# Receptance inputs rounded in four groups spread over the third gate block, longer landings in the recurrence's list, and row loads dealt in pairs

## The chip, the cores and the metric

The kernel runs on one core of a Trainium2 chip. The metric is the device time of one execution in microseconds. The kernel before takes 1137.41 us, the median of three runs (1137.01 to 1139.67).

## The reference

The reference is a layer of a recurrent mixer (RWKV7) followed by a layer of sparse attention, on 256 tokens of width 2048. What matters here is the mixer: six mixed inputs, four large products with weights of 2048x2048 (receptance r, key k, value v, gate z), and a recurrence of each head's 64x64 state over the tokens, with a norm, a bonus and the gate behind it.

```python
xx = token_shift(u) - u
mixed = u[None] + xx[None] * mu[:, None, None, :]
rkvz = jnp.einsum('nbtd,nde->nbte', mixed[:4], w_rkvz)
r, k, v, z = rkvz[0], rkvz[1], rkvz[2], rkvz[3]
...
o = wkv7_scan(rh, heads(decay), kh, vh, -kk, kk * ah.astype(jnp.float32))
mean = jnp.mean(o, axis=-1, keepdims=True)
var = jnp.mean(jnp.square(o - mean), axis=-1, keepdims=True)
o = ((o - mean) * lax.rsqrt(var + GN_EPS)).reshape(B, T, D) * ln_g + ln_b
bonus = jnp.sum((rh * kh * r_k).astype(jnp.float32), axis=-1, keepdims=True) * vh
o = (o + bonus.reshape(B, T, D)) * jax.nn.silu(z)
```

## The kernel before, in words

**Products in two parts.** Each float32 operand of a large product is cut into a high part rounded to the matmul's format and a low part, the rest; three matmuls add up the product. For a weight piece of 128x512, ScalarE makes the high part (`whi`, line 211) and VectorE the low part (`wlo`, line 190). The raw weights (`wraw`, 512 KB, two pieces) come through SP's queue (line 177). There are five raw tiles and five buffers each of `whi` and `wlo`, so splits run up to five pieces ahead of TensorE. A raw tile is loaded again when the low part of its last piece is made.

The mixed inputs are cut in the same way. For r, `split_into` is called sixteen times, once per block k of 128 rows: a high part of 128x256 on ScalarE (line 425, scaled by a tile that holds 1.0, `gate`) and a low part on VectorE (line 426). The gate tile is written by POOL (line 655) once the second gate block is closed, and all sixteen wait for it.

**The stages.** First come v and the small products, then k (278 us), then the gate in blocks of 512 columns: z1 until about 301 us, z2 (`late_z(2)`) until 325 us, z3 until 348 us. TensorE's order there is its own. Each block ends with `close_z`: a tanh, a scale and a product per half (lines 661 to 663) and stores of the result. From 348 us on the recurrence runs in units U = 0 to 7 of four heads, some 24 us each, and between its small matmuls the products of r (lines 1337 and 1340) fill TensorE.

**The list of the recurrence.** A planner, `Deal`, writes out the order on ScalarE, VectorE, POOL and SP by hand before anything runs. Each step has an engine, a duration, the steps it needs and a lag, the time after its end until its result counts as there. TensorE's line of steps is given; a step is due when TensorE will want what hangs on it, and an engine takes the most urgent step that can start. The order fixes what stands behind what on each queue; at run time every queue waits in order. The steps that the change touches or that are spoken of below:
- The 32x32 blocks of an inverse are made in two batches, b = 0 in an earlier stage and b = 1 on POOL, ScalarE and VectorE from 305 us until the recurrence's unit 3. Its tiles are invA, invT, invM and invX, line 823. Its results go to memory by two POOL DMAs, called `("tnd1",)` and `("yvd1",)`, which units 4 to 7 read back.
- `("a", U)`: eight POOL DMAs of 16 KB that load the rows A10 and T00 of unit U (`load_a`, lines 922 and 924). `("y", U)`: eight that load Yb (`load_y`, line 931). Each is one step, so its eight DMAs stand together.
- `("G", U)`: TensorE's first product of unit U's preparation (line 1051); needs a and y.
- S: VectorE copies the state after the first chunk (line 1151), and TensorE multiplies it with `ars` (line 1130). `st` is the statistics of a chunk (lines 1167 and 1169), `rp` POOL's power that makes 1/sqrt(var) (`rg`, line 1180), `nmr`, `v`, `b` what VectorE does with it (lines 1190 to 1194).
- SP loads `spl` (the split inputs of a unit), the rows `vt` and `zt`, `uv`, the raw weights, and three `xl` tiles of the input (line 1559), which lie where invA, invT and invX lay.

A POOL DMA's issue takes POOL's time, and a POOL queue that waits for a store's landing holds everything behind it.

Of the kernel before, what the change touches and what calls it, by code (L numbers as in the profile page):

```python
# [78 lines left out]
ZHOOK = (2, 4)  # L79
QZ = (0, 25, 24, 1, 2, 23, 22, 21, 3, 20, 19, 18, 4, 17, 16, 15, 14, 13, 12, 11, 10)  # L80
# [62 lines left out]
class Weights:  # L143


    def __init__(self, tc, pool, raw_bufs, ahead):
        self.tc = tc
        self.nc, self.pool, self.raw_bufs, self.ahead = tc.nc, pool, raw_bufs, ahead
        self.pieces, self.order, self.loads, self.raw, self.hl = [], [], [], {}, []
        self.loaded = self.split = self.taken = 0  # L150
        self.on_pool = set()
        self.kept_from, self.kept_pool = math.inf, None
        self.due, self.hold = [], False

# [47 lines left out]
    def high(self):  # L202
# [8 lines left out]
        self.nc.scalar.activation(hv, src, AF.Copy)  # L211
# [13 lines left out]
def hybrid_kernel(ctx: ExitStack, tc: tile.TileContext, a: dict, out: bass.AP):  # L225
# [320 lines left out]
    def mixgen():  # L546
        for names in (("w", "a"), ("z",), ("k",), ("r",)):
# [5 lines left out]
            for k in range(NK):  # L553
                for nm in names:
# [5 lines left out]
                    if nm == "r":  # L560
                        if k == 0:
                            yield lambda: "z1" in phase_done
                        split_into(xx[:, k, :], nm, k, gates[1.0])
# [89 lines left out]
    def gate(value):  # L653
        t = ph1.tile([128, 1], F32, name="gate", bufs=1)
        G.memset(t, value)
        gates[value] = t

# [133 lines left out]
    def phase_z1():  # L791
# [11 lines left out]
        gate(1.0)  # L803
        phase_done.add("z1")
# [113 lines left out]
    def load_a(U):  # L918
        for x in range(2):
            for h in range(2):  # L920
# [5 lines left out]
    def load_y(U, eng=G):  # L926
        for x in range(2):
            for h in range(2):
# [5 lines left out]
    def late_z(nb):  # L934
        nonlocal A10, T00, vt, zt
        ps = two()
        for k in range(NK):
            yield from rows_step(ps, "z", k, W.get(), 512)
            if nb == 3:
# [53 lines left out]
    each = [(x, h) for x in range(2) for h in range(2)]  # L993
# [414 lines left out]
    for t, nm in ((0.0, ("spl", 0, 0)), (0.0, ("spl", 0, 1)), (0.0, ("a", 0)), (3000.0, ("y", 0)), (11000.0, ("zd",))):  # L1408
        deal.end[nm] = t
# [8 lines left out]
    for i, (eng, n, fn, _) in enumerate(inv):  # L1418
        nm = ("tnd1",) if i in dones[-2:-1] else ("yvd1",) if i in dones[-1:] else ("iv", i)
        deal.end.pop(nm, None)  # L1420
        dur, lag = {"V": (vcost(n), 0.0), "S": (scost(n), 100.0), "G": (gcost(n) if n else 600.0, 100.0 if n else 3500.0),
# [3 lines left out]
    for U in range(NU):  # L1425
        add = deal.add
        e2 = later("p", U - 2, 3, 2)
        if U:
# [3 lines left out]
            if U in (1, 2):  # L1432
                add(("yz", U), "G", 530.0, lambda U=U: G.memset(Yb[U], 0.0))
            third = ("tnd1",) if U == 4 else None
            add(("a", U), "G", 4500.0, lambda U=U: load_a(U), ("Y", U - 1), third, lag=3500.0)
            add(("y", U), "G", 4500.0, lambda U=U: load_y(U), later("p", U - 3, 3, 1), ("yz", U) if U < 3 else None, ("at", 12 * min(U, 2)),
                ("yvd1",) if U == 4 else None, lag=3500.0)
# [6 lines left out]
        pe(("G", U), 600.0, lambda U=U: prep("G", U), ("a", U), ("y", U), later("M", U - 1, 0), later("M", U - 1, 1))  # L1444
# [606 lines left out]
```

## Time and profile before

| | |
|---|---|
| median of three runs | 1137.41 us |
| the profiled execution's own time | 1138.34 us |
| its span | 1136.2 us |
| TensorE busy | 1103.1 us, 97% |
| VectorE, ScalarE, POOL busy | 860.8, 714.3, 382.2 us |
| z2 and z3 | 301 to 348 us |
| recurrence with r's product | 348 to 560 us |

Times in a profile are microseconds from the start of the span. In the order of time a row gives start, duration, engine, line, operation, output<-inputs, count, and in brackets the idle time of the engine before it and what ended it. PE is TensorE, DVE VectorE, ACT ScalarE, POOL GpSimd; SPq rows are the DMA issues of SP's queue. Matmul rows overlap, so the distance between starts is what counts.

### The profile page before, as it was taken

The page shows a single profiled execution, that of the slowest core. Times are in us where ns is not written, and L with a number is a line of the kernel's source. Part 1 is how long each engine was busy: PE and PEld are TensorE (multiplying, and loading weights), DVE is VectorE, ACT ScalarE, POOL GpSimd, SP SyncE. Part 2 cuts the span into 40 slices and gives each one's busy share as a digit, 9 for nine tenths or more (in the row PEclk, how much of TensorE's full clock was granted, in tenths as well). Part 3 has the DMA queues.
Part 4 walks back from the last instruction along what each step waited for, and adds up shares of the span by engine and source line. Part 5 has one row for each costly group of instructions (what it writes and reads, how often), then busy time and mean ns, then how long its engine had stood idle before and what let it go on. Part 6 is the DMA issues. An engine that isn't in the chain of part 4 may idle for free.

```text
span 1136.2 us, 24517 instructions
## 1 busy us (share of the span) xinstructions
PE 1103.1 (97%) x8880; PEld 936.3 (82%) x8880; DVE 860.8 (76%) x1783; ACT 714.3 (63%) x1696; POOL 382.2 (34%) x488
## 2 busy tenths in 40 slices
PE   8999999999899998999999999999999999999997
PEld 6778899988677777777788888787889988898786
DVE  6999976689958996677667876674576888988564
ACT  5667688867655456565556766564656666666553
POOL 1400057755375555662010010101333435352212
PEclk9999999989999999999999999999999999999999
DMA  6568889876999968765457658585645453848562
GB/s 221 173 192 226 245 216 261 241 214 195 256 272 278 246 162 258 191 181 145 133 179 248 211 167 282 164 292 164 191 138 162 129 139 103 205 116 278 163 199 97
DMA packets 239034, 225.35 MB, mean 198 GB/s; under 512 B 58054, under 2 KB 185334, under 8 KB 238913
## 3 DMA queue, kind: packets, MB, share of 16 engines
q1 hardware_dynamic: 233472, 216.65, 65.1%
q0 software_dynamic: 5440, 7.14, 2.4%
q8 instruction: 70, 1.15, 0.4%
q14 instruction: 52, 0.42, 0.1%
HBM read 200.48 MB, written 23.10 MB: 197 GB/s over the span
## 4 chain that ended last, share of the span: by engine, by line
PE 74%; DVE 10%; DMA 7%; issue 4%; ACT 3%; POOL 1%; SPq 1%; ACTq 0%; POOLq 0%; DVEq 0%
PE bank L586 11%; PE bank L588 11%; PE bank L585 11%; PE bank L1337 5%; PE bank L610 5%; DVE wlo L190 3%; PE bank L611 3%; PE bank L604 2%; PE bank L605 2%; PE bank L606 2%; PE bank L241 2%; DMA wraw<-in_a_w_rkvz_dram 2%; PE bank L1340 2%; PE pair L1359 2%; PE pair L1361 1%
## 5 line engine op out<-in xcount | busy, mean ns | idle before, releaser
L190 DVE TENSOR_TENSOR wlo<-wraw,whi 128x512 fp32r<-128x512 f32 (+2 forms) x616 | 443.0, 736 | 164.9 <-ACT whi L211 162.3
L211 ACT ACTIVATE whi<-wraw 128x512 fp32r<-128x512 f32 (+2 forms) x664 | 399.7, 619 | 226.3 <-PE bank L588 84.9
L586 PE MATMUL bank<-wlo,mx 128*128 128x512 f32 (+3 forms) x576 | 216.2, 377 | 3.0 <-DVE wlo L190 2.0
L588 PE MATMUL bank<-whi,mx 128*128 128x512 f32 (+3 forms) x576 | 214.2, 374 | 0.0
L585 PE MATMUL bank<-whi,mx 128*128 128x512 f32 (+3 forms) x576 | 187.3, 376 | 3.6 <-ACT whi L211 2.4
L586 PEld LDWEIGHTS bank<-wlo,mx 128*128 128x128 f32 x576 | 108.3, 188 | 22.8 <-DVE wlo L190 5.5
L585 PEld LDWEIGHTS bank<-whi,mx 128*128 128x128 f32 x576 | 107.5, 188 | 21.7 <-ACT whi L211 3.5
L588 PEld LDWEIGHTS bank<-whi,mx 128*128 128x128 f32 x576 | 108.4, 188 | 16.1 <-POOL mx L1926 0.4
L1337 PE MATMUL bank<-mx,whi 128*128 128x512 f32 x256 | 101.2, 427 | 0.0
L190 POOL TENSOR_TENSOR wlo<-wraw,whi 128x512 fp32r<-128x512 f32 (+2 forms) x48 | 63.2, 1318 | 110.5 <-ACT whi L211 89.8
L610 PE MATMUL bank<-mx,whi 128*128 128x512 f32 x240 | 86.7, 397 | 0.0
L604 PE MATMUL bank<-mx,whi 128*128 128x256 f32 (+1 forms) x288 | 84.3, 293 | 0.3 <-ACT mx L425 0.3
L605 PE MATMUL bank<-mx,whi 128*128 128x256 f32 (+1 forms) x288 | 82.7, 287 | 0.0
L606 PE MATMUL bank<-mx,wlo 128*128 128x256 f32 (+1 forms) x288 | 82.5, 287 | 0.0
L586 PE MATMUL bank<-wlo,kvh 128*128 128x512 f32 x192 | 76.9, 401 | 0.0
L588 PE MATMUL bank<-whi,kvl 128*128 128x512 f32 x192 | 76.1, 396 | 0.0
L1340 PE MATMUL bank<-mx,wlo 128*128 128x256 f32 x256 | 70.4, 283 | 0.7 <-DVE wlo L190 0.7
L611 PE MATMUL bank<-mx,wlo 128*128 128x256 f32 x256 | 70.5, 285 | 0.2 <-DVE wlo L190 0.2
L585 PE MATMUL bank<-whi,kvh 128*128 128x512 f32 x192 | 67.4, 396 | 0.0
L604 PEld LDWEIGHTS bank<-mx,whi 128*128 128x128 f32 (+1 forms) x288 | 55.6, 193 | 1.3 <-ACT mx L425 0.7
L606 PEld LDWEIGHTS bank<-mx,wlo 128*128 128x128 f32 (+1 forms) x288 | 55.5, 193 | 0.8 <-DVE wlo L190 0.2
L605 PEld LDWEIGHTS bank<-mx,whi 128*128 128x128 f32 (+1 forms) x288 | 55.7, 193 | 0.5
(357 smaller groups left out, 2298.1 us busy)
## 6 DMA issues: line engine op xcount, KB each, us to landing
wraw<-in_a_w_rkvz_dram SPq DMA_DIRECT2D x128, 512.0 KB, 5.6
wraw<-in_kv_w_dram SPq DMA_DIRECT2D x48, 512.0 KB, 4.4
wraw<-in_b_w_in_dram SPq DMA_DIRECT2D x40, 512.0 KB, 4.3
wraw<-in_a_w_o_dram SPq DMA_DIRECT2D x32, 512.0 KB, 4.7
wraw<-in_b_w_o_dram SPq DMA_DIRECT2D x32, 512.0 KB, 4.1
spd<-sp SPq DMA_DIRECT2D x16, 642.0 KB, 5.0
wraw<-in_b_w_in_dram SPq DMA_DIRECT2D x24, 384.0 KB, 3.3
spl<-spd SPq DMA_DIRECT2D x14, 642.0 KB, 6.8
```

The source lines that it names most:

```text
L190: eng.tensor_tensor(lv, src, hv.bitcast(F32), op=OP.subtract)
L211: self.nc.scalar.activation(hv, src, AF.Copy)
L585: PE.matmul(o, mh[:, ts], wh[:, 0, :], start=k == ends[0], stop=False)
L586: PE.matmul(o, mh[:, ts], wl[:, 0, :], start=False, stop=False)
L588: PE.matmul(o, ml[:, ts], wh[:, 0, :], start=False, stop=k == ends[1])
L604: PE.matmul(o, wh[:, s, :], mh, start=k == 0 and first, stop=False, **kw)
L605: PE.matmul(o, wh[:, s, :], ml, start=False, stop=False, **kw)
L606: PE.matmul(o, wl[:, s, :], mh, start=False, stop=k == NK - 1, **kw)
L610: PE.matmul(o, wh[:, s, :], joint[nm, k], start=k == 0, stop=False, **kw)
L611: PE.matmul(o[:, :T], wl[:, s, :], mh, start=False, stop=False, **kw)
L1337: both = lambda: PE.matmul(o, wh[:, s, :], joint["r", k], start=k == 0, stop=k == NK - 1)
L1340: PE.matmul(o[:, :T], wl[:, s, :], mixed["r", k][0], start=False, stop=False)
```

## The change

Two parts.

**The rounding of r.** The gate tile is written by ScalarE itself (`r_gate`, an ACTIVATE of 128x1 with scale 0 and bias 1), four times. Only the sixteen blocks' first, fifth, ninth and thirteenth wait for a new gate. The first gate follows the close of z1. After steps 2, 7 and 12 of z2 the next weight split is marked: its scale is the gate tile instead of the constant 1, so that it reads the tile and the next gate must stand behind it. That gate is written after the step that follows. So z2's splits and the roundings of r are laced. ScalarE, from the close of z1; before (ten more roundings stand ahead of these rows, one after the other):

```order
L425 ACTIVATE mx_4427<-xx,gate 128x256
L425 ACTIVATE mx_4464<-xx,gate 128x256
L211 ACTIVATE whi<-wraw 128x512
L425 ACTIVATE mx_4486<-xx,gate 128x256
L425 ACTIVATE mx_4506<-xx,gate 128x256
L211 ACTIVATE whi<-wraw 128x512
L425 ACTIVATE mx_4546<-xx,gate 128x256
L425 ACTIVATE mx_4564<-xx,gate 128x256
L211 ACTIVATE whi<-wraw 128x512 x12
```

and now:

```order
L663 ACTIVATE gate<-half 128x1
L213 ACTIVATE whi<-wraw 128x512
L428 ACTIVATE mx_4183<-xx,gate 128x256
L428 ACTIVATE mx_4205<-xx,gate 128x256
L428 ACTIVATE mx_4244<-xx,gate 128x256
L213 ACTIVATE whi<-wraw,gate 128x512
L213 ACTIVATE whi<-wraw 128x512
L663 ACTIVATE gate<-half 128x1
L213 ACTIVATE whi<-wraw 128x512
L428 ACTIVATE mx_4264<-xx,gate 128x256
L428 ACTIVATE mx_4288<-xx,gate 128x256
L428 ACTIVATE mx_4305<-xx,gate 128x256
```

The twelve roundings that stood in one block are now in groups of three to five, each behind its gate, with splits between; VectorE's roundings (line 426 before, 429 now) follow in the same groups.

**The list of the recurrence.** The two stores of the inverse count as landed 6.5 us after their issue instead of 3.5. The eight loads of `("a", U)` and of `("y", U)` are four steps of two DMAs each, of 1.12 us and with a lag of 5.5 us, instead of one step of 4.5 us and a lag of 3.5; G waits for all eight steps. The list that comes out differs on ScalarE, VectorE, POOL and SP, and TensorE's is the same. POOL around 426 to 450 us; before (the tnd store and three more pairs of a and t loads stand ahead of these rows):

```order
L922 DMA a_4224<-abd 32x4x32
L924 DMA t_4225<-tnd_1541 32x4x32
L823 DMA yvd_1543<-invX 128x1024
L1042 TENSOR_TENSOR ars_4716<-spl_4704 128x384
L931 DMA Yb_4705<-yvd_1543 32x4x32 x8
L1001 MEMSET uv_4707 64x8x64 x2
L1180 TENSOR_TENSOR rg<-rg,half 128x8
```

and now:

```order
L1191 TENSOR_TENSOR rg<-rg,half 128x8
L831 DMA tnd_1541<-invT 128x1024
L831 DMA yvd_1543<-invX 128x1024
L1053 TENSOR_TENSOR ars_4722<-spl_4710 128x384
L931 DMA a_4224<-abd 32x4x32
L933 DMA t_4225<-tnd_1541 32x4x32
L931 DMA a_4224<-abd 32x4x32
L933 DMA t_4225<-tnd_1541 32x4x32
L939 DMA Yb_4711<-yvd_1543 32x4x32 x4
```

The yvd store stood behind all loads of a(4), of which the t loads wait for the tnd store; now it stands right behind that store, and Yb's loads are laced with those of a(4). VectorE at the first state of unit 3; before:

```order
L1192 TENSOR_TENSOR vt<-vt,bon 128x512
L1190 SCALAR_TENSOR_TENSOR nmr<-mv,rg 128x8
L1194 TENSOR_TENSOR vt<-vt,gb 128x512
L190 TENSOR_TENSOR wlo<-wraw,whi 128x512
L1151 COPY S<-pair_6338 128x128
L1036 TENSOR_TENSOR mb<-mb,spl_4229 128x256
L1167 BN_STATS sta<-pair_6338 128x6 x2
L1169 BN_AGGR mv<-sta 128x2 x2
```

and now:

```order
L1162 COPY S<-pair_6340 128x128
L1203 TENSOR_TENSOR vt<-vt,bon 128x512
L1201 SCALAR_TENSOR_TENSOR nmr<-mv,rg 128x8
L1205 TENSOR_TENSOR vt<-vt,gb 128x512
L1178 BN_STATS sta<-pair_6340 128x6 x2
L1180 BN_AGGR mv<-sta 128x2 x2
```

The copy S stood behind nmr, which waits for POOL's power, and stands ahead of it now. On SP the three `xl` loads, which stood behind the rows of vt and zt, two raw loads and an spl load of unit 3, stand ahead of the vt rows now; and the two copies of invM on ScalarE near z3's end stand ahead of z3's tanh instead of behind it.

```diff
--- before.py
+++ after.py
@@ -77,6 +77,7 @@
 FILLL = (3, 3, 3, 2, 3, 2, 3, 3, 3, 3, 3, 3)
 FILLO, LASTFILL = 4, 28
 ZHOOK = (2, 4)
+RGK, RGZ = (0, 4, 8, 12), (2, 7, 12)
 QZ = (0, 25, 24, 1, 2, 23, 22, 21, 3, 20, 19, 18, 4, 17, 16, 15, 14, 13, 12, 11, 10)
 SQG, XPG, W2G = 0, 1, 0
 ZB = 8
@@ -151,6 +152,7 @@
         self.on_pool = set()
         self.kept_from, self.kept_pool = math.inf, None
         self.due, self.hold = [], False
+        self.mark = {}
 
     def add(self, ap, per, queue=True):
         n, cols = ap.shape[1:]
@@ -208,7 +210,8 @@
         hv, lv = [pool.tile([128, 512], F32R, name=nm, bufs=bufs)[:, :per * cols]
                   .rearrange("p (k c) -> p k c", k=per) for nm in ("whi", "wlo")]
         eng = self.nc.gpsimd if self.split in self.on_pool else self.nc.vector
-        self.nc.scalar.activation(hv, src, AF.Copy)
+        self.nc.scalar.activation(hv, src, AF.Copy, **self.mark)
+        self.mark = {}
         self.due.append((lv, src, hv, eng))
         self.hl.append((hv, lv))
         self.raw[p][1] -= 1
@@ -558,9 +561,9 @@
                         while ("v", k) not in mixed:
                             yield 300.0
                     if nm == "r":
-                        if k == 0:
-                            yield lambda: "z1" in phase_done
-                        split_into(xx[:, k, :], nm, k, gates[1.0])
+                        if k in RGK:
+                            yield lambda: ("r", k) in phase_done
+                        split_into(xx[:, k, :], nm, k, gates["r"])
                     else:
                         mix(nm, k)
                     yield {"w": DW, "a": DW, "k": DK, "z": DZ, "r": DRM}[nm]
@@ -654,6 +657,12 @@
         t = ph1.tile([128, 1], F32, name="gate", bufs=1)
         G.memset(t, value)
         gates[value] = t
+
+    def r_gate(k):
+        t = ph1.tile([128, 1], F32, name="gate", bufs=1)
+        S.activation(t, half[:, 0:1], AF.Copy, scale=0.0, bias=1.0)
+        gates["r"] = t
+        phase_done.add(("r", k))
 
     def close_z(nb, ps, ths, eng):
         for tt in range(2):
@@ -800,8 +809,7 @@
                     if j < NK:
                         part(j)
         close_z(1, ps, [kph.tile([128, 512], F32, name="zth", bufs=2) for _ in range(2)], nc.sync)
-        gate(1.0)
-        phase_done.add("z1")
+        r_gate(RGK[0])
 
     def inverse_load(b):
         A = late.tile([128, 32, 32], F32, name="invA", bufs=1)
@@ -915,17 +923,17 @@
     inverse = lambda d, u, q: bass.AP(tensor=d.tensor, offset=d.offset + (q * 64 + u // 2 * 8 + u % 2) * 1024,
                                       ap=[[32, 32], [2 * 1024, NCH], [1, 32]])
 
-    def load_a(U):
-        for x in range(2):
-            for h in range(2):
+    each = [(x, h) for x in range(2) for h in range(2)]
+
+    def load_a(U, pairs=each):
+        for x, h in pairs:
                 j, at = 2 * U + x, 64 * (h ^ x) + 32
                 G.dma_start(A10[at:at + 32, x, :, 0:32],
                             abd[j, :, 0, 64 * h + 32:64 * h + 64, :].rearrange("c p s -> p c s"))
                 G.dma_start(T00[64 * h:64 * h + 32, x, :, 0:32], inverse(tnd[U // 4], (j % 8) * 2 + h, 0))
 
-    def load_y(U, eng=G):
-        for x in range(2):
-            for h in range(2):
+    def load_y(U, eng=G, pairs=each):
+        for x, h in pairs:
                 for q in range(2):
                     at = 64 * (h ^ x) + 32 * q
                     eng.dma_start(Yb[U % 3][at:at + 32, x, :, 32 * q:32 * q + 32],
@@ -936,6 +944,10 @@
         ps = two()
         for k in range(NK):
             yield from rows_step(ps, "z", k, W.get(), 512)
+            if nb == 2 and k in RGZ:
+                W.mark = dict(scale=gates["r"])
+            elif nb == 2 and k - 1 in RGZ:
+                r_gate(RGK[1 + RGZ.index(k - 1)])
             if nb == 3:
                 used.add(("z", k))
                 if k == ZHOOK[1]:
@@ -990,7 +1002,6 @@
     ones2 = one("ones2", [128, 2])
     PCH, PBK, OU, GY, GS, AT, XS, STA, SST, NRM = [{} for _ in range(10)]
     mm = dict(stop=True, skip_group_check=True)
-    each = [(x, h) for x in range(2) for h in range(2)]
 
     in_order = ExitStack()
     in_order.enter_context(tc.manual_schedule(engines={e.engine for e in (PE, V, S, G, nc.sync)}))
@@ -1405,7 +1416,7 @@
     def pe(nm, dur, fn, *after):
         deal.add(nm, "P", dur, fn, *after, lag=220.0)
 
-    for t, nm in ((0.0, ("spl", 0, 0)), (0.0, ("spl", 0, 1)), (0.0, ("a", 0)), (3000.0, ("y", 0)), (11000.0, ("zd",))):
+    for t, nm in ((0.0, ("spl", 0, 0)), (0.0, ("spl", 0, 1)), *[(t, (s, 0, x, h)) for t, s in ((0.0, "a"), (3000.0, "y")) for x, h in each], (11000.0, ("zd",))):
         deal.end[nm] = t
     for n in range(6, 31):
         deal.end["at", n] = 1000.0 * n
@@ -1418,7 +1429,7 @@
     for i, (eng, n, fn, _) in enumerate(inv):
         nm = ("tnd1",) if i in dones[-2:-1] else ("yvd1",) if i in dones[-1:] else ("iv", i)
         deal.end.pop(nm, None)
-        dur, lag = {"V": (vcost(n), 0.0), "S": (scost(n), 100.0), "G": (gcost(n) if n else 600.0, 100.0 if n else 3500.0),
+        dur, lag = {"V": (vcost(n), 0.0), "S": (scost(n), 100.0), "G": (gcost(n) if n else 600.0, 100.0 if n else 6500.0),
                     "Q": (1000.0, 4500.0)}[eng]
         deal.add(nm, eng, dur, fn, back, lag=lag)
         back = nm if nm != ("tnd1",) else back
@@ -1432,16 +1443,17 @@
             if U in (1, 2):
                 add(("yz", U), "G", 530.0, lambda U=U: G.memset(Yb[U], 0.0))
             third = ("tnd1",) if U == 4 else None
-            add(("a", U), "G", 4500.0, lambda U=U: load_a(U), ("Y", U - 1), third, lag=3500.0)
-            add(("y", U), "G", 4500.0, lambda U=U: load_y(U), later("p", U - 3, 3, 1), ("yz", U) if U < 3 else None, ("at", 12 * min(U, 2)),
-                ("yvd1",) if U == 4 else None, lag=3500.0)
+            for x, h in each:
+                add(("a", U, x, h), "G", 1120.0, lambda U=U, x=x, h=h: load_a(U, [(x, h)]), ("Y", U - 1), third, lag=5500.0)
+                add(("y", U, x, h), "G", 1120.0, lambda U=U, x=x, h=h: load_y(U, G, [(x, h)]), later("p", U - 3, 3, 1),
+                    ("yz", U) if U < 3 else None, ("at", 12 * min(U, 2)), ("yvd1",) if U == 4 else None, lag=5500.0)
         add(("vz", U), "G", 1050.0, lambda U=U: clear_v(U), e2)
         add(("v", U), "Q", 2300.0, lambda U=U: load_v(U), ("vz", U), ("at", 6 + 12 * min(U, 1)), lag=3000.0)
         add(("vt", U), "Q", 1600.0, lambda U=U: load_rows(vt, vd, U), ("at", 26), *[later("+", U - 1, x) for x in range(2)], lag=3000.0)
         add(("zt", U), "Q", 1600.0, lambda U=U: load_rows(zt, zd, U), ("at", 30), *[later("z", U - 1, x) for x in range(2)], lag=3000.0)
         if U % 4 == 0:
             add(("gb", U), "Q", 3600.0, lambda U=U: load_gb(U), ("at", 22), *[later(k, U - 1, x) for k in "gb" for x in range(2)], lag=3000.0)
-        pe(("G", U), 600.0, lambda U=U: prep("G", U), ("a", U), ("y", U), later("M", U - 1, 0), later("M", U - 1, 1))
+        pe(("G", U), 600.0, lambda U=U: prep("G", U), *[(s, U, x, h) for s in "ay" for x, h in each], later("M", U - 1, 0), later("M", U - 1, 1))
         add(("gs", U), "S", scost(256), lambda U=U: prep("gs", U), ("G", U), later("Y", U - 1))
         pe(("Y", U), 620.0, lambda U=U: prep("Y", U), ("gs", U))
         add(("yb", U), "S", 730.0, lambda U=U: prep("yb", U), ("Y", U))
```

## The prediction

> **What bounds the kernel now.** I read the page first, then the waits of TensorE, then the order of time around each wait.
>
> ```profile
> span 1136.2 us, 24517 instructions
> PE 1103.1 (97%) x8880; PEld 936.3 (82%) x8880; DVE 860.8 (76%) x1783; ACT 714.3 (63%) x1696; POOL 382.2 (34%) x488
> ```
>
> TensorE is busy for 1103.1 of 1136.2 us, and the change leaves its list of matmuls in the same order. Nothing can be gained but its idle time, so I looked for the idle time that lies where the change moves work. The waits of TensorE in the windows 301 to 362 us and 362 to 560 us (total, times, longest):
>
> ```profile
> PE bank L585 <- ACT whi L211: 1.9, 2, 1.3
> PE bank L1340 <- DVE wlo L190: 0.7, 1, 0.7
> ...
> PE pair L1130 <- DVE mv L1169: 3.3, 3, 2.9
> ```
>
> Three places, then: the second and third gate blocks (z2 and z3), a low part of a weight at 357 us, and one wait of 2.9 us in the recurrence.
>
> **Place one, z2 and z3.** Order of time on TensorE (start, duration, what ended the idle time):
>
> ```profile
> 306.57 0.62 PE L585 MATMUL bank<-whi,mx 128*128 128x512 f32 x2
> ...
> 307.93 0.62 PE L585 MATMUL bank<-whi,mx 128*128 128x512 f32 x2
> ...
> 310.76 0.73 PE L585 MATMUL bank<-whi,mx 128*128 128x512 f32 x2 [1.31 <-ACT whi L211]
> ...
> 312.52 0.62 PE L585 MATMUL bank<-whi,mx 128*128 128x512 f32 x2
> ...
> 323.44 0.61 PE L585 MATMUL bank<-whi,mx 128*128 128x512 f32 x2
> ...
> 325.54 0.73 PE L585 MATMUL bank<-whi,mx 128*128 128x512 f32 x2 [0.59 <-ACT whi L211]
> ...
> 327.30 0.62 PE L585 MATMUL bank<-whi,mx 128*128 128x512 f32 x2
> ```
>
> A piece of weights takes 307.93 - 306.57 = 1.36 us. From 307.93 to 312.52 lie two pieces, which should take 2.72; they took 4.59, so 1.87 us were lost. From 323.44 to 327.30 it is 3.86 - 2.72 = 1.14. The first loss is ScalarE's, which did twelve roundings in one go before the next split; the second is a late load:
>
> ```profile
> 305.28 4.91 ACT L425 ACTIVATE mx<-xx,gate 128x256 fp32r<-128x256 f32 x12 [0.68 <-POOL gate L655]
> ...
> 312.74 3.37 ACT L211 ACTIVATE whi<-wraw 128x512 fp32r<-128x512 f32 x6
> ...
> 324.86 1.15 ACT L211 ACTIVATE whi<-wraw 128x512 fp32r<-128x512 f32 x2 [6.03 <-DMA wraw<-in_a_w_rkvz_dram]
> ```
>
> After the change a group is at most five roundings. Per piece ScalarE has one split (3.37 / 6 = 0.56) and one rounding (4.91 / 12 = 0.41): 16 x 0.97 = 15.5 us against 16 x 1.36 = 21.8 us of TensorE. The largest group is 5 x 0.41 = 2.05 us, and whi has five buffers, so TensorE has several pieces of 1.36 us in hand. VectorE's sixteen roundings of the same size move with them. The four gates are ACTIVATEs of 128x1; the nearest row is the 128x8 one,
>
> ```profile
> L1183 ACT ACTIVATE bon<-pair 128x8 f32<-128x8 f32 x7 | 1.2, 172 | 0.0
> ```
>
> so 4 x 0.17 = 0.7 us of ScalarE, inside 21.8 - 15.5 = 6.3 us of slack; were that cover gone they would cost 0.7. POOL's memset disappears. So the 1.87 us should go: between 0 and 1.87, I take 1.8.
>
> The second loss hangs on the load queue. A raw tile is loaded again once its last low part is made, and VectorE made those late, behind its roundings. The queue of SP, and its waits from 300 to 330 us:
>
> ```profile
> 304.72 4.55 SPq L278 DMA_DIRECT2D zd<-zth  x4
> 309.36 3.79 SPq L177 DMA_DIRECT2D wraw<-in_a_w_rkvz_dram  x2
> ...
> SPq L177 <- DVE mx L426: 3.6, 2, 2.6
> ```
>
> The second of the two loads of 309.36 went out near 312.8. Without the wait of 2.6 it goes about 2.4 us sooner, at 310.4. But the transfers are full there, and POOL starts its own in the same moment:
>
> ```profile
> 305.00:313.00 8.00, 6.69 (x29) 4.90 (x28) 7.64 (x18) 7.72 (x19) 3.26 (x9) 1.00 1.08 303
> ...
> 320.00:330.00 10.00, 9.41 (x40) 6.94 (x39) 2.59 (x4) 3.28 (x6) 9.21 (x19) 1.00 1.07 263
> ...
> 310.14 1.07 POOL L811 DMA_DIRECT2D invA<-abd  x2 [4.72 <-DMA zd<-zth]
> 311.17 1.16 POOL L956 DMA_DIRECT2D spl<-spd  x2
> ```
>
> A busy share of 1.08 and 1.07 means that an earlier load only passes others. The second load now stands ahead of the two spl loads of 642 KB (1.28 MB at 280 GB/s, between the 303 and 263 of these rows, is 4.6 us), so it lands near 320, and TensorE, 1.87 us ahead, wants it at 322.9. The loads after it have less to pass, and TensorE comes to them early too. Bounds 0 to 1.14; I take 0.6, in all 2.4 us for z2 and z3.
>
> The Trainium skill ("DMA: Bandwidth & Descriptors", "Issuing engines are not separate DMA queues") says that DMAs of all issuing engines run on the same 16 DMA engines and interleave. By that, SP's load would share with spl instead of passing it, the 0.6 would be about 0, and the sum below 0.6 smaller; this agrees with the shares over 1.0, and no row of before shows two orders of the same loads.
>
> **Place two, 357 us.** VectorE did a run of small operations of the inverse (L823) before three low parts in a row:
>
> ```profile
> 356.73 1.89 DVE L190 TENSOR_TENSOR wlo<-wraw,whi 128x512 fp32r<-128x512 f32 x3
> ...
> 357.47 0.39 PE L1340 MATMUL bank<-mx,wlo 128*128 128x256 f32 x1 [0.74 <-DVE wlo L190]
> ```
>
> In the new order low parts stand between those operations. 0 to 0.74; I take 0.6. The same shift puts the two copies of invM on ScalarE ahead of two splits; they wait for POOL, which ended at 345.85 before:
>
> ```profile
> 345.61 0.24 POOL L823 COPY invT<-invM 128x64 f32<-128x64 f32 x1
> 350.18 0.53 ACT L823 ACTIVATE invM<-invT 128x64 f32<-128x64 f32 x2
> ```
>
> TensorE needs those splits about three pieces after z3, near 349.5, so it costs nothing unless POOL ends 3.6 us later (a rival below).
>
> **Place three, the recurrence at 450 us.** POOL's order of time, then VectorE's and TensorE's:
>
> ```profile
> 426.26 0.64 POOL L823 DMA_DIRECT2D tnd<-invT  x1 [0.58 <-DVE nmr L1190]
> ...
> 433.71 0.55 POOL L924 DMA_DIRECT2D t<-tnd  x1 [5.99 <-DMA tnd<-invT]
> ...
> 437.50 0.56 POOL L823 DMA_DIRECT2D yvd<-invX  x1
> ...
> 443.70 4.37 POOL L931 DMA_DIRECT2D Yb<-yvd  x8 [4.25 <-DMA yvd<-invX]
> 448.06 1.12 POOL L1001 MEMSET uv<- 64x512 f32 x2
> 449.26 1.67 POOL L1180 TENSOR_TENSOR rg<-rg,half 128x8 f32<-128x8 f32 x1
> ...
> 450.96 0.17 DVE L1190 SCALAR_TENSOR_TENSOR nmr<-mv,rg 128x8 f32<-128x8 f32 x1 [3.92 <-POOL rg L1180]
> ...
> 452.25 0.29 DVE L1151 COPY S<-pair 128x128 f32<-128x128 f32 x1
> ...
> 447.60 0.45 PE L1137 MATMUL pair<-uv,bkt 128*64 128x64 f32 x8
> ...
> 453.29 0.46 PE L1130 MATMUL pair<-S,ars 64*64 64x64 f32 x16 [2.89 <-DVE mv L1169]
> ```
>
> POOL waits 5.99 us for one store, only then starts the other, and waits 4.25 us again; its power of rg is late, nmr behind it, and the state's copy S behind nmr on VectorE. Now the yvd store stands right behind tnd, so it lands near 436 instead of 443.2 (both are 512 KB; tnd took until 433.1). The eight Yb loads (0.55 each) and the a/t loads between them end near 443.3, and after uv (1.12) and four more Yb loads (2.2) the power (1.67) runs from 446.6 to 448.3. That puts nmr near 448.5, 2.4 us sooner; and the copy S stands ahead of nmr now, with BN_STATS behind it, so TensorE waits for neither. S's operand is made at 447.60 + 0.45 = 448.05, the copy takes 0.29, and TensorE comes at 453.29 - 2.89 = 450.4. The 2.89 us go: 0 to 2.89, I take 2.6. What is late next is G(4), the first user of Yb: its last load lands some 5 us after its issue (a row below has 4.7), near 448.3, against 450.7.
>
> Against it: the loads of unit 1 are dealt in pairs, so that a(1) now comes behind six of y(1)'s and ends issuing at 371.4 instead of 368.4. Loads and user:
>
> ```profile
> a<-abd POOLq DMA_DIRECT2D x5, 16.0 KB, 4.7
> ...
> 378.05 0.84 PE L1051 MATMUL pair<-Yb,a 64*64 64x32 f32 x32
> ```
>
> 371.4 + 4.7 = 376.1, 1.9 us before G(1) at 378.05; both move with TensorE, since POOL's ars ahead of them waits for it through VectorE. With the slowest landing shown below (7.1) it is late by 0.5; between 0 and 0.5 I take the upper end, since G(2) to G(4) meet the same. SP now starts the three xl loads before the rows of vt and zt, and waits for yvd's landing with them. From 436.5 on, 1.5 MB of xl at 280 GB/s (5.6 us) and a landing of 5 put those rows at 447; they are wanted at 448.6, so this costs nothing.
>
> **Sum:** -2.4 - 0.6 - 2.6 + 0.5 = -5.1 us. The profiled execution's own time is 1138.34, 2.1 us around its span, and becomes 1133.2; the median of the runs is 1137.41, and becomes **1132.3 us**. All gains in full: 1.87 + 1.14 + 0.74 + 2.89 = 6.64, so 1130.8. A measurement here tells a change from none at about 0.3%, 3.4 us: faster means below 1134.0.
>
> **Rivals.**
> 1. Transfers take z back. For it: shares of 1.08 and 1.07. Against it: the first 1.87 us are ScalarE's own order, no transfer. If the loads leave TensorE where it was at 327 us, place one gives 0, and -0.6 - 2.6 + 0.5 = -2.7: 1134.7.
> 2. The wait at 450 only changes hands, to Yb's or nmr's late landing in G(4). For it: landings of 16 KB took 4.7 us here and POOL waits for an earlier one at times. Against: 2 us in hand. Then -2.4 - 0.6 + 0.5 = -2.5: 1134.9.
> 3. The new order does nothing for the end, since both come true: 1137.4.
> 4. Slower: POOL's list of single loads becomes the clock of units 1 to 4. If a load lands in 7.1 us instead of 4.7, as such loads did from 304 to 330 us,
>
> ```profile
> a<-abd POOLq DMA_DIRECT2D x4, 16.0 KB, 7.1
> ```
>
> then the second half of 16 loads starts 2.4 late and lands 2.4 later, 4.8 us less 1 to 2 in hand, some 3.3 at each of four G's: +13.2 - 5.6 = +7.6, so 1145. It decides from a landing of about 5.5 us on. Beside it is ScalarE behind invM: one microsecond for each that POOL's inverse ends past 349.5, should spl and invA land behind the raw loads.
>
> **Chances.** Forecast 0.56 (its own range 1130.8 to 1134.2), rival 1 0.15, rival 2 0.12, rival 3 0.08, rival 4 0.09. Below 1134.0 lie most of the forecast (0.53) and a third of rivals 1 and 2 (0.09): faster 0.62; same: 0.03 + 0.18 + 0.07 = 0.28; slower 0.10. The range reaches over rivals 1 and 2 to 1136.6 and down to 1130.4.
>
> **What would show it.** In the new profile: splits between groups of three to five roundings and no wait for whi near 308 us; the wait for a raw load near 323 us at under 0.6; no wait for wlo near 354; POOL's two stores side by side near 423, and a copy S on VectorE ahead of nmr with no wait of TensorE over 0.5 us where unit 3 first uses it. I am wrong if TensorE's idle time comes back at G(1) or G(4), released by a Yb or t load, or if splits stand behind invM.

## The result, and the profile after

The changed kernel takes **1134.15 us**, the median of five runs (1132.56 to 1135.24), against 1138.9 of the kernel before in five runs (1137.01 to 1139.67): a ratio of 0.9943 (0.9925 to 0.9961) as recorded with the runs; the quotient of the two medians is 0.9958. The forecast was 1132.3, with a range of 1130.4 to 1136.6, and faster with a chance of 0.62. It put the bound of faster at 1134.0, 3.4 us under a median of 1137.41. The time is 0.15 above that, but 3.4 us under the 1138.9 of the five runs is 1135.5, and the whole interval of the ratio lies under 0.997. The profiled execution's span is 1130.5 us, 5.7 less than before.

The page:

```profile
span 1130.5 us, 24527 instructions
PE 1101.1 (97%) x8880; PEld 933.9 (83%) x8880; DVE 862.0 (76%) x1783; ACT 714.7 (63%) x1700; POOL 379.5 (34%) x487
```

The waits of TensorE (total, times, longest), first from 301 to 362 us, then from 362 to 560 us, then from 462 to 700 us:

```profile
...
PE bank L588 <- ACT whi L213: 0.3, 1, 0.3
...
PE pair L1062 <- DMA Yb<-yvd: 0.9, 1, 0.9
PE pair L1141 <- issue: 0.8, 2, 0.6
...
PE bank L1685 <- ACT whi L213: 0.7, 1, 0.7
```

The three waits of the prediction (1.3 and 0.6 for whi, 0.7 for wlo, 2.9 in the recurrence) are gone or down to 0.3. New are a wait of 0.9 for a Yb load, three waits with no releaser ("issue": the two of the row above, and one of 0.3 at line 1103), and 0.7 for a split of a later stage at 682 us.

Since TensorE's list is the same in both kernels, each matmul can be set against its twin. This gives how far a kernel is ahead of the profile of before at a given time of it, so the difference of two columns is what a stage gave. (The kernels in the lower rows are told below; the columns are the times of before.)

| us ahead at | 300 | 350 | 365 | 448 | 462 | 520 | 700 |
|---|---|---|---|---|---|---|---|
| changed kernel | 1.5 | 3.8 | 4.7 | 3.2 | 4.9 | 6.5 | 5.4 |
| the same again | 1.4 | 3.7 | 4.6 | 4.4 | 0.8 | 1.6 | 1.4 |
| rounding alone | 0.9 | 3.3 | 4.1 | 2.2 | 3.2 | 3.3 | 2.8 |
| list alone | 0.8 | 1.9 | 2.8 | 3.4 | 5.9 | 4.1 | 4.1 |
| list alone, xl held | 2.2 | 2.6 | 3.6 | 3.4 | 6.1 | 5.9 | 6.3 |
| change, xl held (first) | 0.3 | 3.2 | 3.3 | 3.6 | 6.1 | 6.8 | 7.1 |
| change, xl held (again) | 0.0 | 2.4 | 3.3 | 3.6 | 6.2 | 6.9 | 7.3 |

The first column is chance. Up to 300 us ScalarE, VectorE, POOL and SP work in the same order in all these kernels, and yet they are 0.0 to 2.2 us ahead: 1.5 of the 5.7 us between the two profiles are no effect of the change.

**z2 and z3.** ScalarE, then TensorE, then the second load of SP (start, time to its landing):

```profile
309.39 0.73 ACT L213 ACTIVATE whi<-wraw,gate 128x512 fp32r<-128x512 f32 x1 [0.72 <-DVE wlo L192]
310.14 0.20 ACT L663 ACTIVATE gate<-half 128x1 f32<-128x1 f32 x1
310.38 1.71 ACT L428 ACTIVATE mx<-xx,gate 128x256 fp32r<-128x256 f32 x4
...
319.59 0.72 ACT L213 ACTIVATE whi<-wraw,gate 128x512 fp32r<-128x512 f32 x1 [4.13 <-DMA wraw<-in_a_w_rkvz_dram]
...
320.58 2.11 ACT L428 ACTIVATE mx<-xx,gate 128x256 fp32r<-128x256 f32 x5
322.60 0.61 ACT L213 ACTIVATE whi<-wraw 128x512 fp32r<-128x512 f32 x1
...
341.62 0.54 ACT L831 ACTIVATE invM<-invT 128x64 f32<-128x64 f32 x2 [0.33 <-POOL invT L831]
...
323.26 0.73 PE L588 MATMUL bank<-whi,mx 128*128 128x512 f32 x2 [0.32 <-ACT whi L213]
...
308.85 10.63 DMA wraw<-in_a_w_rkvz_dram
```

The second load lands at 319.5 instead of 324.8, and what is left is one wait of 0.32 for the split at 322.60, which stands behind the group of five roundings. A gate costs 0.20, four 0.8, near the 0.7 of the sum. The copies of invM wait 0.33 for POOL, and TensorE has no wait there.

**The recurrence.** POOL, SP, VectorE and TensorE:

```profile
425.04 0.64 POOL L831 DMA_DIRECT2D tnd<-invT  x1
427.52 0.54 POOL L831 DMA_DIRECT2D yvd<-invX  x1 [1.83 <-ACT bon L1194]
...
432.16 1.39 SPq L1571 DMA_DIRECT2D xl<-in_x_dram  x3
...
433.41 2.17 POOL L939 DMA_DIRECT2D Yb<-yvd  x4
...
440.75 0.55 POOL L931 DMA_DIRECT2D a<-abd  x1 [1.93 <-DMA Yb<-yvd]
...
441.89 1.09 POOL L939 DMA_DIRECT2D Yb<-yvd  x2
...
446.26 1.67 POOL L1191 TENSOR_TENSOR rg<-rg,half 128x8 f32<-128x8 f32 x1
...
445.37 0.29 DVE L1162 COPY S<-pair 128x128 f32<-128x128 f32 x1 [0.15 <-PE pair L1121]
...
447.95 0.80 DVE L1201 SCALAR_TENSOR_TENSOR nmr<-mv,rg 128x8 f32<-128x8 f32 x1 [1.69 <-POOL rg L1191]
...
449.28 0.35 DVE L1178 BATCH_NORM_STATS2 sta<-pair 128x6 f32<-128x64 f32 x2
...
447.14 0.46 PE L1141 MATMUL pair<-S,ars 64*64 64x64 f32 x16
...
448.64 0.62 PE L1062 MATMUL pair<-Yb,a 64*64 64x32 f32 x26 [0.85 <-DMA Yb<-yvd]
```

S's product starts at 447.14 without a wait, though BN_STATS still stands behind nmr and comes 2.1 us later, at 449.28. But the product with Yb, 0.3 us behind it, stops after six of its matmuls and waits 0.85: the last two of the eight Yb loads, issued from 441.89 on, landed at 448.3 and 448.5. SP's three xl loads, 1.5 MB, went out at 432.2, just ahead of Yb's loads, and POOL waits 1.93 between them.

These late landings hold POOL as well. In this row of sixteen loads the twelfth and the thirteenth go out just after the landings of the fourth and the fifth (437.99 and 440.47), so that eight are under way at most. POOL's power starts at 446.26. The kernel is 3.2 us ahead at this place, and the power of before started at 449.26, so for TensorE it comes 0.2 us later than before, not sooner.

### The profile page after: what moved, and what is told of

Its sections match the earlier page's. It is cut to its first block, busy times and chain, and to the rows that moved or that the text cites. A ratio compares the mean times of both kernels' runs of the same rounds, so it can differ in the third digit from the quotient of the medians.

```text
span 1130.5 us, 24527 instructions
## 1 busy us (share of the span) xinstructions
PE 1101.1 (97%) x8880; PEld 933.9 (83%) x8880; DVE 862.0 (76%) x1783; ACT 714.7 (63%) x1700; POOL 379.5 (34%) x487
## 3 DMA queue, kind: packets, MB, share of 16 engines
q8 instruction: 70, 1.15, 0.5%
## 4 chain that ended last, share of the span: by engine, by line
PE 71%; DVE 10%; DMA 5%; POOL 5%; issue 4%; ACT 3%; SPq 0%; POOLq 0%; ACTq 0%; DVEq 0%
PE bank L589 11%; PE bank L591 11%; PE bank L588 11%; PE bank L1348 6%; PE bank L613 5%; DVE wlo L192 3%; POOL sp L764 3%; PE bank L614 3%; PE bank L1351 3%; PE bank L244 2%; DMA wraw<-in_a_w_rkvz_dram 2%; PE pair L1370 2%; DMA spd<-sp 2%; PE pair L1372 1%; PE pair L1371 1%
## 5 line engine op out<-in xcount | busy, mean ns | idle before, releaser
L607 PE MATMUL bank<-mx,whi 128*128 128x256 f32 (+1 forms) x288 | 83.0, 288 | 0.3 <-ACT mx L428 0.3
L608 PE MATMUL bank<-mx,whi 128*128 128x256 f32 (+1 forms) x288 | 81.4, 283 | 0.0
L1348 PEld LDWEIGHTS bank<-mx,whi 128*128 128x128 f32 x256 | 47.6, 188 | 10.5
L607 PEld LDWEIGHTS bank<-mx,whi 128*128 128x128 f32 (+1 forms) x288 | 54.2, 188 | 1.3 <-ACT mx L428 0.7
```

The source lines that it names most:

```text
L607: PE.matmul(o, wh[:, s, :], mh, start=k == 0 and first, stop=False, **kw)
L608: PE.matmul(o, wh[:, s, :], ml, start=False, stop=False, **kw)
L1348: both = lambda: PE.matmul(o, wh[:, s, :], joint["r", k], start=k == 0, stop=k == NK - 1)
```

## The experiments

**The two parts apart.** The rounding part alone leaves the list's three edits out:

```diff
-        "G": (..., 100.0 if n else 6500.0)
+        "G": (..., 100.0 if n else 3500.0)
-            for x, h in each:
-                add(("a", U, x, h), "G", 1120.0, ...
+            add(("a", U), "G", 4500.0, lambda U=U: load_a(U), ("Y", U - 1), third, lag=3500.0)
```

> The rounding part alone; stores and loads of the recurrence's list as before. Theory: z2 and z3 give back about 2.3 us (no wait for whi near 309 us, the wait for a late raw load near 325 us at 0.3), the wait of 0.7 us for wlo near 357 us and the wait of 2.9 us near 450 us stay as they were, and the first 300 us are as before: some 2.3 us less than the kernel before. Rival (the transfers take it back): the loss near 325 us grows by what the first wait gave, and the time is that of before. Rival (the 1.4 us that the changed kernel was ahead at 300 us come from the change): TensorE is ahead by 1 us or more at 300 us here too.

It took 1137.76 against 1138.99, 0.999 (0.9976 to 1.0004). By the table it gave 2.3 us from 300 to 350 us, as expected. It also gave 0.8 at 357, where the wait for wlo was expected to stay, and its wait near 450 us was 1.7, not 2.9. From 365 to 448 us it lost 1.9 again, with a wait of 0.7 without a releaser and one of 0.7 for statistics. The rival of the transfers falls: the loss near 325 us fell to 0.3 too. The timing alone can't tell 2 us from nothing.

The list's part alone puts all roundings behind POOL's one gate again:

```diff
-                        if k in RGK:
-                            yield lambda: ("r", k) in phase_done
+                        if k == 0:
+                            yield lambda: "z1" in phase_done
```

> The list's part alone (longer landing of the two stores, loads in pairs); the roundings of r in one block behind POOL's gate. Theory: z2 and z3 lose their 3 us as before; near 450 us the wait of 2.9 us becomes one of about 0.9 us for a Yb load, the wait for wlo near 357 us is gone (1 us), the small waits of TensorE for statistics between 477 and 516 us are gone (1.1 us), and some 1.5 us are lost between 366 and 390 us: 1.5 to 3 us less than before. Rival (the two parts need each other, since the roundings shift the inverse and so the list): less than 0.5 us is gained and the wait near 450 us stays over 2 us.

1134.02 against 1138.99, 0.9963 (0.9951 to 0.9975), 4.2 us: more than expected. The wait for whi near 309 us is there (1.1), those for wlo and in the recurrence are gone, and the two parts don't need each other. The expected wait for Yb did not come: the last Yb load landed at 447.4. That the wait for wlo went both with the rounding part alone and with the list alone shows that either shift of VectorE's order is enough.

**Spread or other engine.** One gate, written by ScalarE:

```diff
-RGK, RGZ = (0, 4, 8, 12), (2, 7, 12)
+RGK, RGZ = (0,), ()
```

> The changed kernel with the gate written by ScalarE once, behind z1, and all sixteen roundings behind that one gate; the list as in the changed kernel. Theory (the spreading is what helps): ScalarE does a block of roundings again and TensorE waits for whi over 1 us near 309 us, as before. Rival (it is the gate's engine, POOL's memset being late): no wait over 0.5 us near 309 us, as in the changed kernel.

One run, 1131.82, too few for a verdict on its time. From 300 to 350 us it gave 0.9, against 2.3 with four groups. ScalarE did ten roundings in a row, and the wait was between the two expectations:

```profile
305.43 4.09 ACT L428 ACTIVATE mx<-xx,gate 128x256 fp32r<-128x256 f32 x10
...
310.09 0.73 PE L588 MATMUL bank<-whi,mx 128*128 128x512 f32 x2 [0.55 <-ACT whi L213]
```

Kernels with all roundings behind POOL's gate were themselves 0.4 to 1.1 us faster there than the profile of before (five profiles, 0.6 in the mean), since the late load near 325 us cost them less. So the spreading is worth about 1.9 us, not 2.3: the six profiles that have it gave 2.3 to 3.1, 2.6 in the mean.

**The longer landing alone.**

```diff
-        "G": (..., 100.0 if n else 3500.0)
+        "G": (..., 100.0 if n else 6500.0)
```

> The kernel before with the longer landing of the two stores alone; loads whole, roundings in one block. Theory (the stores' order and the state's copy ahead of nmr are what removes the 2.9 us): yvd stands two steps behind tnd and the copy S ahead of nmr, so the wait near 450 us falls below 1.2 us and the time is 1.5 to 3 us less than before. Rival (the pairs are needed, since a whole y behind a whole a lands too late): TensorE waits 1.5 us or more for a Yb load there, and the time is within 1 us of before.

1140.7 against 1138.99, 1.0011 (0.9996 to 1.0026): my theory falls, and so does the rival of a late Yb load. VectorE copied S ahead of nmr, as I wanted, and TensorE still waited:

```profile
448.75 0.28 DVE L1158 COPY S<-pair 128x128 f32<-128x128 f32 x1
452.10 0.17 DVE L1197 SCALAR_TENSOR_TENSOR nmr<-mv,rg 128x8 f32<-128x8 f32 x1 [3.07 <-POOL rg L1187]
...
452.52 0.36 DVE L1174 BATCH_NORM_STATS2 sta<-pair 128x6 f32<-128x64 f32 x2
...
453.03 0.70 PE L1137 MATMUL pair<-S,ars 64*64 64x64 f32 x16 [3.25 <-DVE mv L1176]
```

S was there at 449.0. The wait ends with the statistics BN_STATS and their mean, behind nmr. They read the tile of PSUM that TensorE's next product writes (other columns of it), and the list wrote them down ahead of that product.

**Whether it is the statistics.** The same kernel, with a chunk's statistics put behind TensorE's next product in the list; VectorE's order at this place stays:

```diff
-            add(("st", U, c), "V", 800.0, ..., ("p", U, c, 2), ...
+            add(("st", U, c), "V", 800.0, ..., ("p", U, c, 2), ("p", U, c + 1, 0) if c < NCH - 1 else None, ...
```

> The kernel with only the longer landing of the two stores (in which VectorE copies S ahead of nmr, but TensorE still waits 3.3 us near 450 us), and with each chunk's statistics written down behind TensorE's next product; VectorE's own order at that place is the same. Theory (TensorE waits for the statistics BN_STATS, which stand behind nmr and were written down ahead of its product, and not for S): the wait near 450 us falls below 0.5 us, and the small waits of 0.2 to 0.4 us at the other units' first states are gone. Rival (it waits for S or for a load): the wait stays over 2 us.

TensorE, then VectorE:

```profile
450.55 0.46 PE L1137 MATMUL pair<-S,ars 64*64 64x64 f32 x16
...
452.66 0.17 DVE L1197 SCALAR_TENSOR_TENSOR nmr<-mv,rg 128x8 f32<-128x8 f32 x1 [3.58 <-POOL rg L1187]
...
453.08 0.36 DVE L1174 BATCH_NORM_STATS2 sta<-pair 128x6 f32<-128x64 f32 x2
```

POOL's power is as late as before, and S's product starts without a wait 2.5 us ahead of the statistics, so these were what it had waited for. A wait of 1.3 comes behind it, for X, and ends at 453.9:

```profile
PE pair L1140 <- ACT X L1151: 1.3, 1, 1.3
...
```

and waits of 0.3 to 0.6 for late statistics come at four other products. One run, 1137.43.

**Pairs alone.** The landing of 6.5 us is taken out instead, and the roundings stay in one block:

```diff
-            add(("a", U), "G", 4500.0, lambda U=U: load_a(U), ("Y", U - 1), third, lag=3500.0)
+            for x, h in each:
+                add(("a", U, x, h), "G", 1120.0, ..., ("Y", U - 1), third, lag=5500.0)
```

> The kernel before with the loads dealt in pairs (and their longer landing) alone; the two stores count as landed after 3.5 us as before, so that yvd stands behind the loads of a(4) again, and VectorE's copy S behind nmr. Theory (both halves of the list's part are needed): TensorE waits 2 us or more near 450 us as in the kernel before, and the time is within 2 us of before. Rival (the pairs alone do it): the wait is under 1.2 us and the time 3 us or more less than before.

1136.37 against 1139.62, 0.9967 (0.9947 to 0.9988). The theory falls: yvd stood behind a(4)'s loads again, but POOL's power came ahead of the memset of uv, and the wait for the statistics was 1.19. By its letter the rival holds (under 1.2, and 3.3 us less), but the gain does not lie there. From 448 to 462 us this profile lost 0.8, since the clock (third from the end of these rows) fell behind the wait:

```profile
450.00:453.00 3.00, 2.74 (x44) 1.99 (x43) 0.69 (x1) 1.73 (x6) 1.45 (x3) 0.81 1.00 171
453.00:456.00 3.00, 3.00 (x29) 2.39 (x29) 1.39 (x3) 1.86 (x5) 2.48 (x6) 0.62 0.90 247
```

By the times the pairs alone give as much as both edits of the list (0.9967 and 0.9963), and the longer landing alone gives nothing. What the longer landing adds is shown in the profiles alone: 2.5 us from 448 to 462 us with both.

**The same kernel again.** No edit.

> The changed kernel as it is, once more, beside the next ones on the same chip. Theory: 5 to 6 us less than the kernel before; the wait for a Yb load near 448 us is there again (0.6 to 1.2 us), while the waits inside a row of equal matmuls near 373 to 387 us, for which the profile names no releaser, stand elsewhere or nowhere. Rival (those waits come from the dealt loads): they stand near 373 to 387 us again, 1 us in sum.

1134.28 against 1140.25, 0.9953 (0.9934 to 0.9972). Its profiled execution, though, has a span of 1135.2, 4.7 us more than the first one's, and loses 3.6 us from 448 to 462 us, where the first gained 1.7. The stretches from 447 on (TensorE's busy time, ..., granted clock, DMA share, GB/s), of the first execution and of this one:

```profile
447.00:450.00 3.00, 2.15 (x54) 1.68 (x52) 1.89 (x6) 0.96 (x4) 3.00 (x5) 1.00 1.11 303
450.00:453.00 3.00, 3.00 (x59) 2.43 (x61) 0.06 (x1) 2.96 (x12) 1.75 (x5) 1.00 1.23 238
```

```profile
447.00:450.00 3.00, 1.51 (x30) 1.14 (x30) 1.90 (x6) 0.90 (x4) 2.58 (x4) 0.89 1.13 295
450.00:453.00 3.00, 2.87 (x17) 2.42 (x17) 0.00 (x0) 2.96 (x12) 2.23 (x6) 0.50 1.25 187
453.00:456.00 3.00, 3.00 (x59) 2.52 (x58) 0.89 (x2) 0.59 (x2) 0.00 (x0) 0.50 0.91 170
```

Third from the end of a row is the granted clock. Here TensorE waited 1.15 for Yb and, after 1.5 us of work, 0.89 for X. After that its clock was 0.50 until about 459 us, and that costs more than the waits. The waits with no releaser weren't near 380 us again; one of 0.58 stood at 507.

**The xl loads held.** Each waits for a small copy from a later result, so that they start near 490 us:

```diff
         xl = xlp.tile([128, 2, 512], F32, name="xl", bufs=3)
+        if nb < 3:
+            G.tensor_copy(xl[:, 0, 0:16], mixed["y", (6, 6, 6)[nb]][0][:, 0:16].bitcast(F32))
```

> The changed kernel with the three xl loads held until after unit 4 (each waits for a small copy from a later result). Theory (the xl loads, 1.5 MB, pass in front of Yb's and make them land 7 us after issue): Yb's loads near 434 us land in 5 us or less, POOL's waits between them go, the wait for Yb near 448 us (0.9 us and some slow matmuls behind it) is gone: 1 us less than the changed kernel. Rival (Yb lands late because its own sixteen loads hold one another): landings stay at 6 to 7 us and the wait stays.

1130.65 against 1140.25, 0.9925 (0.9909 to 0.9941), and 3.6 us less than the changed kernel beside it, where 1 us was expected. Yb's loads issued from 433 to 440 us took 6.8 us to land (median) in the changed kernel, the same again 7.9, and here 4.0:

```profile
Yb<-yvd POOLq DMA_DIRECT2D x6, 16.0 KB, 6.8
```

```profile
Yb<-yvd POOLq DMA_DIRECT2D x5, 16.0 KB, 7.9
```

```profile
spl<-spd SPq DMA_DIRECT2D x1, 642.0 KB, 6.7
Yb<-yvd POOLq DMA_DIRECT2D x8, 16.0 KB, 4.0
```

TensorE's waits from 362 to 520 us in this kernel are a single row:

```profile
PE pair L1141 <- issue: 0.5, 1, 0.5
```

So the xl loads in front were what made Yb late. In the three profiles with this hold (two are told next) the median is 3.9 to 4.1, in the four with xl in front and Yb in pairs 6.4 to 7.9. But late is not always too late. With 6.4, in the list alone, the last Yb load landed at 447.4 and TensorE did not wait; and here the last two of the eight still took 7.5, issued just behind the spl load of the row above, and landed at 447.3.

The same kernel once more, and beside it one with the same hold and the one gate and block of roundings of before, that is, the list's part alone with xl held:

> The changed kernel with the xl loads held, once more, beside the one without the spread roundings. Theory: some 8 us less than the kernel before (0.992 to 0.994), full clock near 450 us. Rival: the earlier time was luck, and it is that of the changed kernel, 5 to 6 us less than before.

> The list's part with the xl loads held until after unit 4, and the roundings of r in one block as before. With the same kernel plus the spread roundings beside it, this prices the rounding part where no wait near 450 us and no lower clock behind it blurs the times. Theory: no wait over 0.5 us near 450 us, z2 and z3 lose 2 to 3 us as before, so 6 us less than the kernel before and 2 us more than the kernel beside it. Rival (the rounding part is worth nothing, since the loads take it back): the two are within 0.5 us.

0.9937 (0.9923 to 0.9952) and 0.9938 (0.992 to 0.9956): 1132.93 and 1131.69 against 1140.22. Both beat the changed kernel's ratio, though the intervals overlap. The times don't tell the two apart, but the profiles do in their place: 2.4 us against 0.4 from 300 to 350 us. The second profile was 2.2 us luckier before 300 us, which is the size of the effect. So the rounding part's 2 us are shown in their stage; no comparison of times shows them, here or in the rounding alone.

**Both at once.** The two edits above, xl held and statistics behind the next product, on the changed kernel, which I thought best:

> The changed kernel with the xl loads held and each chunk's statistics written down behind TensorE's next product. Theory: 1 to 2 us less than the changed kernel, 6 to 8 us less than the kernel before; no wait over 0.5 us between 392 and 520 us but those inside a row of equal matmuls. Rival: POOL or VectorE take it back at another unit, and the time is that of the changed kernel.

1138.65, 0.9989 (0.9976 to 1.0001): the rival holds. POOL's power came late (449.2), ScalarE's normalisation O, which waits for nmr, stands ahead of X, and TensorE waits for X:

```profile
451.71 0.70 ACT L1215 ACTIVATE O<-pair,nmr,rg 128x64 f32<-128x64 f32 x2 [4.02 <-DVE nmr L1201]
452.67 0.28 ACT L1155 ACTIVATE X<-pair 128x128 f32<-128x128 f32 x1 [0.27 <-DVE mv L1180]
```

The stretch behind it, with the granted clock third from the end:

```profile
453.00:456.00 3.00, 3.00 (x17) 2.42 (x17) 0.00 (x0) 2.96 (x11) 0.03 (x1) 0.50 0.04 5
```

The wait was 2.9 us, and the clock 0.50 behind it. It only changed hands. What POOL waited for ahead of its power (3.24, without a releaser) stays open.

## Why the prediction was right, and where its steps were not

- **z2 and z3, -2.4.** 2.3 was measured, and the way was the predicted one: no block of roundings, the second load 5 us sooner. Some 0.6 of it is that the profile of before was a bad execution there; the edit itself is worth about 1.9. Rival 1, that the transfers take it back, did not come. The load went out at 308.85 instead of 312.78, ahead of both spl loads (309.73 and 310.31), and landed ahead of them, as worked out from the order of issue (319.5, "near 320"). But the order of issue does not tell it all: SP's next load, issued at 309.37 and so ahead of spl too, landed at 322.6, behind the first spl load (320.3). The Trainium skill's rule ("DMA: Bandwidth & Descriptors", "Issuing engines are not separate DMA queues"), that the transfers of all engines interleave, agrees with that and with Yb's late landings behind xl. That by it the 0.6 would be about 0 did not come true: the load went out 3.9 us sooner, 1.5 of it by chance, and took 10.6 us instead of 12.0.
- **357 us, -0.6.** From 350 to 365 us 0.7 to 1.0 was measured in every profile with the pairs but the first with xl held, where a wait of 0.6 for wlo stayed. The rounding alone gave 0.8 with the old list, so low parts between the inverse's operations are not the only way to it. POOL's inverse ended at 341.6, so the rival at ScalarE's invM had no ground.
- **450 us, -2.6.** The first profile gave 1.7, the second lost 3.6; with xl held it was 2.5 to 2.7 in three profiles. So the size was right for the edit by itself. Three steps were wrong. "SP now starts the three xl loads ... so this costs nothing" looked only at the rows behind xl on SP, and not at Yb's loads on POOL's queue, which land 2 to 4 us later behind 1.5 MB. That is the wait of rival 2, put at 0.12, together with the forecast's gain, and by the prediction's own sign ("I am wrong if TensorE's idle time comes back at G(1) or G(4), released by a Yb or t load") it was wrong there. "That puts nmr near 448.5, 2.4 us sooner" did not come either: POOL stood behind the same late loads, and for TensorE its power was 0.2 us later than before. And "the copy S stands ahead of nmr" is not why TensorE goes on. With S ahead of nmr and the statistics written down ahead of the product it waited 3.25 (the longer landing alone); with them written down behind it, it did not wait. In the changed kernel the product starts 2.1 us ahead of the statistics. That the new list had moved them too is what made the gain, and the prediction did not see it.
- **G(1) to G(4), +0.5.** From 365 to 448 us the other kernels with the pairs lost or gained 0.1 to 0.6, except the last one, which lost 2.4 with waits of 1.0 and 0.8 for late statistics. The changed kernel's first profile lost 1.5, of which 1.1 are waits with no releaser. G(1) cost 0.5 for an a load in the second profile and 0.3 in another. Rival 4 stayed away.
- **Not in the sum:** 462 to 520 us gave 1.6 in the first profile and 0.7 in its second one and in the two with xl held, each with a wait of 0.5 to 0.6 without a releaser in it: the small waits for statistics of before (0.6 and 0.4 in sum, the rows below) went with the new order; 520 to 700 us cost 1.1, by a wait of 0.7 for a split at 682 us that the second execution had at 0.3. The waits for statistics in the profile of before, from 462 to 700 us:

```profile
PE pair L1130 <- DVE sta L1167: 0.6, 2, 0.4
PE pair L1130 <- DVE mv L1169: 0.4, 2, 0.2
```

In the first profile the stages from 300 to 700 us give 2.3 + 0.9 - 1.5 + 1.7 + 1.6 - 1.1 = 3.9 us, and the 1.5 ahead of them are chance. The total of -5.1 came true within its uncertainty, partly by luck: a missed gain (the small waits for statistics) and a missed loss (Yb behind xl) have opposite signs.

## What to carry to other kernels

A list that starts one store earlier also lets go what waited for its landing: look for transfers on every queue that the earlier landing releases, not only for the consumers one has in mind, since they pass in front of the next loads. And TensorE's wait for a tile of PSUM ended here with the last reader that the list had written down before the product, so the reader's place in the list decides, not only the operand's. Where single microseconds count, set each matmul against its twin and read the stages: two executions of one program differed by 4.7 us here.

## What the runs showed of the hardware

**The clock falls after short waits.** After 3.25 us of waiting (the kernel with the longer landing alone) TensorE's granted clock was 0.50 for some 6 us, and the matmuls took 2.6 us more. After 1.15 and 0.89 with 1.5 us of work between (the same kernel again) they took 4.1 more than in the first execution; after 1.70 in the list alone, 1.5 more; after 1.19 and 0.16 in the pairs alone, 1.5 more. But after 2.89 in the profile of before, and 1.70 in the rounding alone, the clock stayed 1.00. The stretches of before behind its wait of 2.89 us (TensorE busy for 0.40 of 3 us, and the clock still 1.00), then that of the rounding alone with its wait of 1.70, then those of the longer landing alone and of the list alone behind their waits:

```profile
450.00:453.00 3.00, 0.40 (x3) 0.08 (x1) 2.04 (x7) 1.80 (x6) 3.00 (x5) 1.00 1.08 299
453.00:456.00 3.00, 2.71 (x65) 2.30 (x66) 1.03 (x5) 2.73 (x10) 2.15 (x5) 1.00 1.30 238
...
447.00:450.00 3.00, 1.30 (x16) 0.92 (x18) 2.39 (x9) 2.23 (x8) 3.00 (x6) 1.00 1.07 302
...
454.00:456.00 2.00, 2.00 (x25) 1.52 (x21) 0.00 (x0) 1.38 (x5) 0.91 (x4) 0.50 0.36 79
...
504.00:506.00 2.00, 2.00 (x8) 1.42 (x6) 1.97 (x4) 0.86 (x3) 1.75 (x4) 0.53 0.21 36
```

The Trainium skill, "TensorE: Matmul & The Clock Gate", section "What's actually happening", tells of a free-running window of about 3.4 us and of a half clock after an idle one. That the same wait is punished or not agrees with a window that runs freely; that two waits of 2.04 us in sum were enough, and of 1.35 in the pairs alone, does not agree with a window that must be idle throughout. What share of a window counts was not tried.

**Waits inside a row of equal matmuls.** Rows such as this one, in the list alone, stand in the middle of sixteen products of the same operands and have no releaser. Nine of the eleven profiles of a changed list have one of 0.3 to 1.7 us in the same row of sixteen products, at 502 to 512 us. The first of the changed kernel has three from 373 to 387 us instead, the kernel with one gate has none, and that of before has none from 300 to 700 us.

```profile
503.69 0.33 PE L1137 MATMUL pair<-S,ars 64*64 64x64 f32 x5 [1.70 <-issue]
```

What TensorE's sequencer waits for there stays open.
